# First merge's products, the gates and the head splits moved into the planned part of a hybrid RWKV-7 and GDN layer

## The chip, the cores and the metric

The kernel runs on one core of one Trainium2 chip. The metric is the device time of one execution in microseconds. Engines are named PE (TensorE), DVE (VectorE), ACT (ScalarE), POOL (GpSimd) and SP (SyncE, which here only issues DMAs).

## The reference

One layer over 256 latent tokens x and 256 context tokens ctx, of width 2048, in fp32. Both are normed and modulated by rows of an adaLN product (c with a 2048 x 12288 matrix), go through one input projection, and then through two token mixers: RWKV-7 (16 heads of 64, in both directions) and a gated DeltaNet (GDN; 8 heads of 128, chunks of 64, in both directions). Context only gives the scans their first state. Then the merge, the projection and the FFN:

```python
h = modulate(rmsnorm(x, norm1_w), sh1, sc1); hc = modulate(rmsnorm(ctx, norm1_w), csh1, csc1)
o_a = rwkv_readout(scans over h @ w_in, started from those over hc @ w_in)
o_b = gdn_readout(scans over h @ w_in, started from those over hc @ w_in)
g_a, g_b = split(h @ w_in[gate columns])
m = sigmoid(g_a) * (o_a @ p_a) + sigmoid(g_b) * (o_b @ p_b)
x = x + gt1 * (m @ w_out)
x = x + gt2 * swiglu(modulate(rmsnorm(x, norm2_w), sh2, sc2), w_gate_up, w_down)
return rmsnorm(x, final_norm_w)
```

## The kernel before

**Products.** Each big fp32 product is three in fp32r: the weights are loaded (`wraw`), ACT casts them to `whi`, DVE subtracts to get `wlo`, and PE multiplies whi with the high and the low part of the activations and wlo with the high part. A block of weights is 128 columns by 2048 rows, in four quarters of 256 KB (128 partitions x 512). Of such blocks there are 24 for the RWKV pairs (k, r, v for each of 8 pairs of heads), 24 for the GDN heads (K, V, Q), and 40 gates "g" (8 for the GDN readout, 32 for the merge).

**Stages.** (1) Norms, adaLN's first blocks and modulation write h: `H2` (line 441), two tiles (high, low) that hold latent and context tokens side by side, so that a product over both has 512 columns (k, v, K, V) and one over the latents 256 (r, Q, g). (2) A part whose order is planned: RWKV pairs (grams, inverse, values, scan), then GDN heads (features, tokens, decays, grams, inverse, scan), with the products as filling between. (3) First merge: p_a's 16 products (lines 1680 to 1696). (4) Second merge: p_b's 16 (lines 1705 to 1716). (5) w_out, FFN, last norm.

**What sets the order.** In (2) the class `Weave` writes the order of PE, DVE, ACT and POOL by a table of costs (`Lane.product`, line 117): pieces of work are generators with a rank, and where PE would have to wait for a chain's step the next of the products stands there. `products()` keeps the list of blocks; GATES_A and GATES_B say how many gates come free after each RWKV pair and each head. A block's weights are asked for at the start of the product before it (`weights`, `fetch`, `cast`). SP's row, all loads with few exceptions, is put in order by the scheduler; SP takes it in order, and a load waits there until its buffer is free. Inverses turn their blocks by storing to DRAM and loading again (`scr`, `tscr`; stores of LT, iv and extra).

**adaLN's rest** (`ada_rest`, `row_tile`): 80 tiles of 512 KB in two buffers `aw`, loaded by POOL's queue (`g.dma_start`), each added to `acc` by two instructions of 128x512 on DVE (150 in all, ten more on ACT); after 16 tiles a sum `ada_sum` goes through PE. The second merge begins behind these in PE's row, with some of its products ahead of the last sum.

**Merge.** Gates are written to DRAM (`gts_`, line 1143) and loaded again as one tile of 4 MB (line 1690) after the last one; ACT takes their sigmoid (line 1695) while p_a's products run, POOL multiplies the first merge's results with the first 16 (line 1712), DVE the second's with the others (line 1714).

## Time and profile before

| | us |
|---|---|
| median of 3 runs | 2246.44 |
| least and most of them | 2244.85, 2249.73 |
| profiled execution, time | 2257.04 |
| its span | 2254.4 |
| PE busy in it | 2132.3 |
| DVE busy in it | 1552.8 |
| ACT busy in it | 1120.9 |
| POOL busy in it | 102.1 |

The profile is of one execution; its span runs from the first to the last instruction, and 2.6 us lie around it. In its rows an engine's line number is the line of the kernel, but nearly all that the planner writes has line 160, where `Weave` records an operation; there a group is known by its tiles, out first ("wlo<-wraw,whi"). Busy times of matmuls overlap one another, since they are pipelined; their spacing, not their length, says what they cost. A clock of 0.98 is the share of full speed that was granted to PE.

### The profile page before, as it was taken

To read this page: it belongs to the slowest core of one execution; us is meant where nothing else is said; L and a number is where in the kernel's file an instruction comes from. 1 tells how busy PE (TensorE), PEld (TensorE's weight loads), DVE (VectorE), ACT (ScalarE), POOL (GpSimd) and SP (SyncE) were. 2 spreads that over 40 slices of the span, in tenths; PEclk is the share of its full clock that TensorE was granted. 3 is DMA by queue.
4 is the path that set the end of the run, shared out by engine and by line. 5 is a ranking of instruction groups with operands and counts; after the bars stand their busy time and mean duration, and the time that the engine had idled before them with its cause. 6 is when DMAs were issued, how large, how long until landed. Compare 5 with 4: busy or idle time off the path is not lost.

```text
span 2254.4 us, 55503 instructions
## 1 busy us (share of the span) xinstructions
PE 2132.3 (95%) x22906; PEld 1906.1 (85%) x22906; DVE 1552.8 (69%) x3245; ACT 1120.9 (50%) x2157; POOL 102.1 (5%) x167
## 2 busy tenths in 40 slices
PE   7998999899999999999999888999999999999998
PEld 4776677678888777888888887989999999999997
DVE  3457588888888668898887767665666665545554
ACT  3246554456545666565654463454444444444443
POOL 0000000000000001111110040000000000000000
PEclk9999999899999999999999898999999999999999
DMA  9966765454443425556667965663777776666665
GB/s 385 414 164 192 203 171 136 121 144 127 112 126 107 105 70 155 157 169 174 181 179 238 292 224 196 216 214 119 241 238 240 237 241 225 196 188 196 193 194 165
DMA packets 260253, 430.83 MB, mean 191 GB/s; under 512 B 117920, under 2 KB 133280, under 8 KB 255648
## 3 DMA queue, kind: packets, MB, share of 16 engines
q1 hardware_dynamic: 234656, 360.17, 51.5%
q0 software_dynamic: 11520, 41.95, 6.1%
q10 hardware_dynamic: 13824, 25.17, 3.5%
q8 instruction: 179, 2.93, 0.5%
q14 instruction: 74, 0.61, 0.1%
HBM read 401.44 MB, written 25.77 MB: 190 GB/s over the span
## 4 chain that ended last, share of the span: by engine, by line
PE 74%; DMA 10%; DVE 7%; ACT 5%; issue 3%; SPq 0%; ACTq 0%; DVEq 0%; POOL 0%; POOLq 0%
PE mm L160 22%; PE mm L433 12%; PE mm L431 12%; PE mm L432 12%; PE s L160 7%; PE pa L160 4%; PE pi L160 2%; DVE arena L160 2%; DVE wlo L160 1%; DMA wr<-wgu 1%; DMA wraw<-w 1%; PE mm L524 1%; DMA gts<-gts__1373 1%; ACT arena L160 1%; DMA aw<-ada_rest 1%
## 5 line engine op out<-in xcount | busy, mean ns | idle before, releaser
L422 DVE TENSOR_TENSOR wlo<-wraw,whi 128x1024 fp32r<-128x1024 f32 x328 | 394.3, 1203 | 319.9 <-ACT whi L421 319.2
L421 ACT CAST whi<-wraw 128x1024 fp32r<-128x1024 f32 x328 | 337.5, 1029 | 467.3 <-PE mm L432 404.9
L160 PE MATMUL mm<-hxh,wlo 128*128 128x256 f32 (+1 forms) x1376 | 462.9, 336 | 9.4 <-DVE wlo L160 9.3
L160 PE MATMUL mm<-hxh,whi 128*128 128x256 f32 (+1 forms) x1376 | 461.4, 335 | 5.9 <-ACT whi L160 5.4
L160 PE MATMUL mm<-hxl,whi 128*128 128x256 f32 (+1 forms) x1376 | 463.4, 337 | 1.2 <-issue 1.2
L433 PE MATMUL mm<-hfh,wlo 128*128 128x256 f32 x1344 | 372.1, 277 | 0.9 <-DVE wlo L422 0.8
L431 PE MATMUL mm<-hfh,whi 128*128 128x256 f32 x1344 | 371.2, 276 | 0.0
L432 PE MATMUL mm<-hfl,whi 128*128 128x256 f32 x1344 | 371.2, 276 | 0.0
L160 PEld LDWEIGHTS mm<-hxh,wlo 128*128 128x128 f32 x1376 | 263.4, 191 | 40.5 <-DVE wlo L160 14.2
L160 PEld LDWEIGHTS mm<-hxh,whi 128*128 128x128 f32 x1376 | 263.2, 191 | 29.4 <-ACT whi L160 6.1
L160 ACT CAST whi<-wraw 128x512 fp32r<-128x512 f32 x344 | 209.9, 617 | 156.8 <-PE mm L160 97.5
L160 PEld LDWEIGHTS mm<-hxl,whi 128*128 128x128 f32 x1376 | 263.1, 191 | 25.9 <-issue 5.2
L160 DVE TENSOR_TENSOR wlo<-wraw,whi 128x512 fp32r<-128x512 f32 x344 | 236.9, 691 | 68.7 <-ACT whi L160 64.4
L433 PEld LDWEIGHTS mm<-hfh,wlo 128*128 128x128 f32 x1344 | 252.4, 188 | 2.4 <-DVE wlo L422 2.2
L431 PEld LDWEIGHTS mm<-hfh,whi 128*128 128x128 f32 x1344 | 252.5, 188 | 0.0
L432 PEld LDWEIGHTS mm<-hfl,whi 128*128 128x128 f32 x1344 | 252.5, 188 | 0.0
L431 PE MATMUL mm<-za,whi 128*128 128x256 f32 x512 | 141.5, 276 | 0.0
L433 PE MATMUL mm<-za,wlo 128*128 128x256 f32 x512 | 141.3, 276 | 0.0
L432 PE MATMUL mm<-za,whi 128*128 128x256 f32 x512 | 141.3, 276 | 0.0
L160 DVE TENSOR_TENSOR arena<-arena 128x512 f32<-128x512 f32 (+17 forms) x522 | 121.7, 235 | 27.4 <-DMA arena<-scr 16.2
L160 DVE SCALAR_TENSOR_TENSOR aw<-aw,ck 128x512 f32<-128x512 f32 x150 | 110.0, 745 | 16.3 <-DMA aw<-ada_rest 9.9
L432 PEld LDWEIGHTS mm<-za,whi 128*128 128x128 f32 x512 | 96.1, 188 | 0.0
(364 smaller groups left out, 3940.4 us busy)
## 6 DMA issues: line engine op xcount, KB each, us to landing
wraw<-w SPq DMA_DIRECT2D x344, 256.0 KB, 3.2
wraw<-wgu SPq DMA_DIRECT2D x168, 512.0 KB, 4.6
aw<-ada_rest POOLq DMA_DIRECT2D x80, 512.0 KB, 4.8
aw<-ada_first SPq DMA_DIRECT2D x32, 1024.0 KB, 11.5
wraw<-wdn SPq DMA_DIRECT2D x64, 448.0 KB, 3.6
wraw<-wout SPq DMA_DIRECT2D x32, 512.0 KB, 4.4
aw<-ada_gt ACTq DMA_DIRECT2D x64, 256.0 KB, 5.2
wraw<-wdn SPq DMA_DIRECT2D x32, 512.0 KB, 3.6
```

The source lines that it names most:

```text
L160: return Op(self, cost, lambda: getattr(self.engine, name)(out, *a, **k), mode, base)
L421: S.copy(hi[:, c, :M], raw[:, c, :M])
L422: V.tensor_sub(lo[:, c, :M], raw[:, c, :M], hi[:, c, :M].bitcast(F32))
L431: E.matmul(ps, hi, Xh[:, k, :n], start=first and i == 0, stop=False)
L432: E.matmul(ps, hi, Xl[:, k, :n], start=False, stop=False)
L433: E.matmul(ps, lo, Xh[:, k, :n], start=False, stop=last and i == len(wt) - 1)
L524: E.matmul(ps[32 * g:32 * g + 32, 0:P], ckr[:, k].rearrange("p a b -> p (a b)"), aws[e, c][:, i, g], start=k == 0, stop=k == KT - 1)
```

## The change

h is kept in four tiles (latent and context, high and low: tags xh, xl, ch, cl) instead of two. A product over both kinds of tokens is now two of 256 columns with the same weights. The four tiles' memory is used again one by one: when the last K and V are done, the context's two become the first merge's inputs and results (`merge_in`: `oa` and `PA`); when the last gate is done, the latents' two become the gates (`merge_gates`: two loads of 2 MB); after p_a's last product the input becomes the GDN heads' output (`merge_heads`, head by head).

In the planned part now stand: p_a's 16 products as kind "p" (two quarters of 128x512 each, where it was 128x1024), their copies from PSUM, the gates' sigmoid, and POOL's products with them in eight pieces of 128x512. Weights are asked for at each quarter, when fewer than four quarters are ahead, instead of only at a block's start; at the last quarter of a product the next block is taken even if its turn has not come ("sure"), and then waited for. 33 of the gates may be taken from the start, three after the grams of head 6, four after those of head 7. After the last RWKV grams every third cast to wlo goes to POOL (52 of 128x512 in all). adaLN's tiles are loaded by SP's queue. x's load of 2 MB (`x1`) and the second merge's code stay where they were.

The core of the diff (the modulation's writes to the new tiles, left out, only follow their names):

```diff
@@ -25,7 +25,7 @@
-GATES_A, GATES_B = ((8, 2, 0, 2, 5, 3, 3, 0), (5, 0, 0, 0, 0, 2, 6, 4))
+GATES_A, GATES_B = ((33,0,0,0,0,0,0,0),(0,0,0,0,0,0,3,4))
@@ -116,6 +116,8 @@
+        if a[0].dtype == F32R and n == T:
+            return 0.1145, "full"
         if a[0].dtype == F32R:
             return 0.0065 + 0.000443 * n, "full"
@@ -439,9 +441,9 @@
-    hx = hx_ctx.enter_context(tc.tile_pool(name="hx", bufs=1, side="right"))
-    H2 = (hx.tile([P, KT, 2, T], F32R, name="hxh"), hx.tile([P, KT, 2, T], F32R, name="hxl"))
-    HX = tuple(t.rearrange("p k a t -> p k (a t)") for t in H2)
+    hx = hx_ctx.enter_context(tc.tile_pool(name="hx", bufs=1, side="right", reuse_waits="tile"))
+    HX, HC = (tuple(hx.tile([P, KT, T], F32R, tag=a + b, name="h" + a + b) for b in "hl") for a in "xc")
+    H2 = tuple(zip(HX, HC))
...
@@ -568,8 +570,11 @@
-                    gemm(ps[:m, :n], [(2 * e + k, w[k][0][:, o:o + m], w[k][1][:, o:o + m])], HX, n,
-                         e == 0 and k == 0, e == NE - 1 and k == 1)
+                    hi, lo = (t[:, o:o + m] for t in w[k])
+                    todo = [(a, w_, X) for w_, part in ((hi, 0), (hi, 1), (lo, 0)) for a, X in enumerate(H2[part][:n // T])]
+                    for i, (a, w_, X) in enumerate(todo):
+                        E.matmul(ps[:m, T * a:T * a + T], w_, X[:, 2 * e + k, :], start=e == k == i == 0,
+                                 stop=e == NE - 1 and k == 1 and i == len(todo) - 1)
@@ -1141,34 +1146,91 @@
         yield s.copy(g, ps[:, :T])
         weave.release(mmb)
         Q.dma_start(gts_[j], g)
+        if j == 39:
+            weave.ready("gates")
     def fetch(src, i):
-        for q in range(NQ):
+        for q in range(src.shape[1] // CG):
             raw = yield raws
             landed[i, q] = raw, weave.now + dq(raw, src[:, CG * q:CG * q + CG, :])
             weave.ready("asked", i, q)
             yield 0.0
-    def cast(i):
-        for q in range(NQ):
+    def cast(i, nq):
+        for q in range(nq):
             yield "asked", i, q
             raw, at = landed.pop((i, q))
             yield max(0.0, at - weave.now)
             hi = yield his
             yield s.copy(hi, raw)
             lo = yield los
-            yield v.tensor_sub(lo, raw, hi.bitcast(F32))
+            late.append(0)
+            yield (g if ("grams", NPAIR - 1, 1) in weave.done and (len(late) % 3 == 0) else v).tensor_sub(lo, raw, hi.bitcast(F32))
             raws.put(raw)
             casts[i, q] = hi, lo
             weave.ready("cast", i, q)
     def weights(src, i):
         weave.add(LAT['crank'], fetch(src, i))
-        weave.add(LAT['crank'], cast(i))
-    casts = {}
+        weave.add(LAT['crank'], cast(i, src.shape[1] // CG))
+    casts, late = {}, []
+    OA, OB, PA, gts = [], [], [], []
+    def both(dst, src, i, n):
+        yield s.copy(dst[0][:, i:i + n], src)
+        yield v.tensor_sub(dst[1][:, i:i + n], src, dst[0][:, i:i + n].bitcast(F32))
+    def merge_in():
+        yield "out", NPAIR - 1
+        for what in "KV":
+            yield what + "gemm", NGH - 1
+        oa = hx.tile([P, 2, 8, T], F32R, tag="ch", name="oa")
+        OA.extend((oa[:, 0], oa[:, 1]))
+        PA.append(hx.tile([P, KT, T], F32, tag="cl", name="PA"))
+        yield dq(PA[0][:, 0:8], oad.rearrange("k p t -> p k t"))
+        for i in range(0, 8, 2):
+            yield from both(OA, PA[0][:, i:i + 2], i, 2)
+        weave.ready("merge")
+    def first_merge(j, ps, last):
+        yield s.copy(PA[0][:, j], ps[:, :T])
+        weave.release(mmb)
+        weave.ready("evicted", j)
+        if last:
+            weave.ready("merged")
+    def merge_gates():
+        yield ("sides",)
+        yield ("gates",)
+        for i, tag in enumerate(("xh", "xl")):
+            gts.append(hx.tile([P, KT, T], F32, tag=tag, name="gts"))
+            w = dq(gts[i], gts_[8 + KT * i:24 + KT * i].rearrange("j p t -> p j t"))
+        yield w
+        yield "gram", NGH - 1
+        for t in gts:
+            for j in range(0, KT, 2):
+                yield s.activation(t[:, j:j + 2], t[:, j:j + 2], AF.Sigmoid)
+        yield s.preload_act_table_set(LNEXP)
+        for j in range(0, KT, 2):
+            for i in (j, j + 1):
+                yield "evicted", i
+            yield g.tensor_mul(PA[0][:, j:j + 2], PA[0][:, j:j + 2], gts[0][:, j:j + 2])
+    def merge_heads():
+        yield ("merged",)
+        t = hx.tile([P, 2, 8, T], F32R, tag="ch", name="ob2")
+        OB.extend((t[:, 0], t[:, 1]))
+        for h in range(NGH):
+            yield "gout", h
+            yield from both(OB, ob[:, h:h + 1], h, 1)
     def products():
@@ -1186,44 +1248,66 @@
         todo += [("g", p, ("prepared", p - 1, 0) if p else None) for p in range(NPAIR) for _ in range(GATES_A[p])]
         todo += [("g", h, ("gram", h)) for h in range(NGH) for _ in range(GATES_B[h])]
+        todo += [("p", j, ("merge",)) for j in range(KT)]
         def choose():
             for i, (what, p, need) in enumerate(todo):
                 if need is None or weave.done.get(need, 1e9) <= weave.now:
-                    return todo.pop(i)[:2]
+                    return todo.pop(i)
         def source(what, p):
+            if what == "p":
+                return A["pa"][p]
             return A["w128"][48 + p if what == "g" else 3 * p + "kvr".index(what) if what in "kvr" else 24 + 3 * p + "KVQ".index(what)]
-        i, nxt = 0, None
-        while todo or nxt:
-            if nxt is None:
+        i, asked, ahead = 0, 0, []
+        def ask(more, sure=False):
+            nonlocal asked
+            while todo and sum(2 if x[0] == "p" else NQ for x in ahead) < more:
                 nxt = choose()
+                if nxt is None and sure and not ahead:
+                    nxt = todo.pop(0)
                 if nxt is None:
-                    yield 0.5
-                    continue
+                    return
                 if nxt[0] == "g":
-                    nxt = "g", next(gate_next)
-                weights(source(*nxt), i)
-            what, p = nxt
-            nxt = choose()
-            if nxt is not None:
-                if nxt[0] == "g":
-                    nxt = "g", next(gate_next)
-                weights(source(*nxt), i + 1)
+                    nxt = "g", next(gate_next), None
+                weights(source(*nxt[:2]), asked)
+                ahead.append(nxt)
+                asked += 1
+        while todo or ahead:
+            ask(1)
+            if not ahead:
+                yield 0.5
+                continue
+            what, p, need = ahead.pop(0)
+            ask(NQ)
+            if need is not None:
+                yield need
             ps = yield mmb
-            n = 512 if what in "kvKV" else T
-            for k in range(KT):
+            sides = ((0, OA),) if what == "p" else ((0, HX), (1, HC))[:1 + (what in "kvKV")]
+            nk = OA[0].shape[1] if what == "p" else KT
+            for k in range(nk):
                 if k % CG == 0:
+                    ask(NQ, k == nk - CG)
                     yield "cast", i, k // CG
                     hi, lo = casts.pop((i, k // CG))
-                for j, (w, x) in enumerate(((hi, HX[0]), (hi, HX[1]), (lo, HX[0]))):
-                    yield e.matmul(ps[:, :n], w[:, k % CG], x[:, k, :n], start=k + j == 0, stop=k == KT - 1 and j == 2)
+                for j, (w, part) in enumerate(((hi, 0), (hi, 1), (lo, 0))):
+                    for a, X in sides:
+                        yield e.matmul(ps[:, T * a:T * a + T], w[:, k % CG], X[part][:, k, :], start=k + j + a == 0,
+                                       stop=k == nk - 1 and j == 2 and a == len(sides) - 1)
                 if k % CG == CG - 1:
                     his.put(hi)
                     los.put(lo)
             i += 1
+            if what != "p" and not any(x[0] != "p" for x in todo + ahead):
+                weave.ready("sides")
             if what == "g":
                 weave.add(150, gate_out(rs, p, ps))
+            elif what == "p":
+                weave.add(150, first_merge(p, ps, not todo and not ahead))
             else:
                 (hd if what in "KVQ" else pr)[p][what + "ps"] = ps
                 weave.ready(what + "gemm", p)
@@ -1632,8 +1716,7 @@
-            yield g.dma_start(w, A["ada_rest"][b, :, k, :])
-            yield 5.2
+            yield dq(w, A["ada_rest"][b, :, k, :])
@@ -1669,53 +1752,37 @@
         for h in range(NGH):
             for i, piece in enumerate((head_scan, head_inverse, head_grams, decays, tokens, features)):
                 weave.add(100 + 10 * h + i, piece(h))
+        weave.add(140, merge_in())
+        weave.add(300, merge_gates())
+        weave.add(99, merge_heads())
         weave.add(500, ada_early())
         weave.add(500, ada_rest())
         weave.tensor = e
         weave.free[e] = FIRST
         weave.run()
     rk_ctx.close()
-    hx_ctx.close()
     wstep[0] = 8
-    gates_ctx = ExitStack()
-    gp = gates_ctx.enter_context(tc.tile_pool(name="gp", bufs=1, reuse_waits="tile", side="right"))
-    PA = gp.tile([P, KT, T], F32, name="PA")
-    Q.dma_start(PA[:, 0:8], oad.rearrange("k p t -> p k t"))
-    Oa = (gp.tile([P, 8, T], F32R, name="oah"), gp.tile([P, 8, T], F32R, name="oal"))
-    for i in range(8):
-        split(Oa[0][:, i, :], Oa[1][:, i, :], PA[:, i, :])
-    gts = gp.tile([P, 32, T], F32, name="gts")
-    Q.dma_start(gts, gts_[8:40].rearrange("j p t -> p j t"))
-    for j in range(KT):
-        ps = pst(pmm, "mm")
-        gemm(ps[:, 0:T], load_w(A["pa"][j], P, 8), Oa, T)
-        S.copy(PA[:, j], ps[:, 0:T])
-        tc.keep_in_program_order(S.activation(gts[:, 2 * j:2 * j + 2, :], gts[:, 2 * j:2 * j + 2, :], AF.Sigmoid))
-    tc.keep_in_program_order(S.preload_act_table_set(LNEXP))
+    PA = PA[0]
     x1p = Places(None, arena, ("x1", KT * T, 1), ("rs", T, 1), ("ssum", T, 1), ("graw", 64, 1), ("s2", 16, 1), ("pad", 176, 1),
                  ("cb", 2048, 1), ("sq", T, 3), ("m", T, 2))
     x1 = x1p.tile([P, KT, T], F32, name="x1")
     ssum = x1p.tile([P, T], F32, name="ssum")
     Q.dma_start(x1, A["xT"])
-    for i in range(8):
-        split(Oa[0][:, i, :], Oa[1][:, i, :], ob[:, i, :])
     m_ctx = ExitStack()
     mp = m_ctx.enter_context(tc.tile_pool(name="mp", bufs=1, reuse_waits="tile"))
     M = (mp.tile([P, KT, T], F32R, name="mh"), mp.tile([P, KT, T], F32R, name="ml"))
     for j in range(KT):
         ps = pst(pmm, "mm")
-        gemm(ps[:, 0:T], load_w(A["pb"][j], P, 8), Oa, T)
-        G.tensor_mul(PA[:, j], PA[:, j], gts[:, j])
+        gemm(ps[:, 0:T], load_w(A["pb"][j], P, 8), OB, T)
         m = x1p.tile([P, T], F32, tag="m", name="m")
-        V.tensor_mul(m, ps[:, 0:T], gts[:, 16 + j])
+        V.tensor_mul(m, ps[:, 0:T], gts[1][:, j])
         V.tensor_add(m, m, PA[:, j])
         split(M[0][:, j], M[1][:, j], m)
-    gates_ctx.close()
+    hx_ctx.close()
     zap = ent(tc.tile_pool(name="zap", bufs=1, reuse_waits="tile", side="right"))
     W4 = zap.tile([P, 2, 4, KT, P], F32R, tag="za", name="w4")
     w4 = []
```

What this does to the order is shown at three places. First PE near the last RWKV steps (R, VX, Pm and LAl are small tiles of the scan; mm is a block's PSUM tile; hx, hc latents and context; rows are instructions in order, "x4" four alike). Before:

```order
L160 MATMUL s<-R_10507,Tx 64x64 x4
L160 MATMUL s<-VX,C 64x128 x2
L160 MATMUL s<-LAl,VX 64x64 x4
L160 MATMUL mm<-hxh,whi 128x512
L160 MATMUL mm<-hxl,whi 128x512
L160 MATMUL mm<-hxh,wlo 128x512
```

And now, the same step:

```order
L162 MATMUL s<-R_12347,Tx 64x64 x4
L162 MATMUL s<-VX,C 64x128 x2
L162 MATMUL s<-LAl,VX 64x64 x4
L162 MATMUL mm<-hch,whi 128x256
L162 MATMUL mm<-hxl,whi 128x256
L162 MATMUL mm<-hcl,whi 128x256
L162 MATMUL mm<-hxh,wlo 128x256
L162 MATMUL mm<-hch,wlo 128x256
```

Each product of 512 columns stands as two of 256, latents then context, and a step of the scan can now stand between the two.

Second SP's row among the heads (`scr` and `tscr` are stores and loads of an inverse, `wraw` weights, `aw` adaLN's tiles). Before:

```order
L171 DMA scr_111<-LT 64x4x64 x2
L171 DMA wraw<-w 128x512
L171 DMA scr_111<-iv 64x4x64 x2
L171 DMA wraw<-w 128x512
L171 DMA arena<-scr_111 64x16x16
L171 DMA wraw<-w 128x512 x5
L1143 DMA gts__1373<-arena 128x256
L171 DMA wraw<-w 128x512 x7
L171 DMA tscr_113<-arena 64x16x16
```

And now, at the corresponding inverse:

```order
L173 DMA scr_114<-LT 64x4x64 x2
L173 DMA scr_114<-extra 64x4x64 x2
L173 DMA wraw<-w 128x512
L173 DMA arena<-scr_114 64x16x16
L173 DMA wraw<-w 128x512 x4
L173 DMA aw<-ada_rest 128x1024 x2
L173 DMA wraw<-w 128x512 x2
L173 DMA aw<-ada_rest 128x1024 x2
L173 DMA wraw<-w 128x512 x3
L173 DMA tscr_116<-arena 64x16x16
```

adaLN's tiles, which were on POOL's queue, now stand between the weights and the inverse's own transfers.

Third PE around the scan of head 7 (TF, keg and gvt are tiles of a head's scan; oah, oal, oa the first merge's input, ob the GDN heads' output). Before:

```order
L431 MATMUL mm<-oah,whi 128x256
L432 MATMUL mm<-oal,whi 128x256
L433 MATMUL mm<-oah,wlo 128x256
L431 MATMUL mm<-oah,whi 128x256
L160 MATMUL s<-TF_10639,keg 128x128 x8
L432 MATMUL mm<-oal,whi 128x256
```

And now:

```order
L162 MATMUL mm<-oa,whi 128x256 x2
L162 MATMUL mm<-oa,wlo 128x256
L162 MATMUL s<-TF_12476,keg 128x128 x4
L162 MATMUL s<-gvt,TF_12476 128x128 x2
L433 MATMUL mm<-ob_18198,whi 128x256 x2
L434 MATMUL mm<-ob_18198,whi 128x256
L435 MATMUL mm<-ob_18198,wlo 128x256
```

The first merge's products end within that scan, and the second merge's (on `ob`) begin in it.

4 lines of the change are left out of this document (2 added, 2 removed).

## The prediction

> **What bounds the kernel now.** I read the page first: who is busy, and what the chain that ended last is made of.
>
> ```profile
> span 2254.4 us, 55503 instructions
> PE 2132.3 (95%) x22906; PEld 1906.1 (85%) x22906; DVE 1552.8 (69%) x3245; ACT 1120.9 (50%) x2157; POOL 102.1 (5%) x167
> PEclk9999999899999999999999898999999999999999
> PE 74%; DMA 10%; DVE 7%; ACT 5%; issue 3%; SPq 0%; ACTq 0%; DVEq 0%; POOL 0%; POOLq 0%
> ```
>
> TensorE (PE) is busy for 95% of the span and holds 74% of the chain, and the change leaves the arithmetic as it is. So it can gain only where PE waits or its granted clock is low. The windows show where, and that the two go together (columns: stretch, length, busy time of PE, weight load, DVE, ACT and POOL, granted clock, DMA share, GB/s). The stretches are, in order: the RWKV pairs (three rows), the heads up to the last inverse, the last head's inverse up to its scan, that scan up to the last adaLN sum, and the second merge's rest (two rows).
>
> ```profile
> 150.00:450.00 300.00, 273.66 (x3187) 208.13 (x3187) 225.14 (x512) 157.68 (x365) 9.68 (x24) 0.94 0.58 167
> 450.00:750.00 300.00, 290.45 (x4560) 241.02 (x4556) 252.23 (x631) 167.27 (x450) 8.13 (x23) 0.98 0.45 119
> 750.00:850.00 100.00, 95.05 (x1143) 74.29 (x1142) 65.48 (x159) 61.67 (x143) 4.21 (x4) 0.99 0.32 91
> 850.00:1212.00 362.00, 354.02 (x3835) 306.28 (x3834) 320.06 (x860) 219.47 (x477) 44.57 (x65) 0.99 0.60 173
> 1212.00:1308.00 96.00, 79.16 (x871) 75.30 (x870) 64.44 (x148) 40.16 (x83) 11.43 (x20) 0.87 0.86 287
> 1308.00:1382.00 74.00, 58.56 (x448) 55.33 (x447) 51.76 (x82) 37.60 (x61) 23.56 (x25) 0.89 0.67 231
> ```
>
> From 150 to 850 PE idles 26.3 + 9.6 + 5.0 = 41 us, and the clock takes 0.06 x 300 + 0.02 x 300 + 0.01 x 100 = 25 us more: 66 us that further work could fill. From 850 to 1212 it idles 8 us in 362: dense. From 1212 to 1382 it idles 16.8 + 15.4 = 32 us, and the clock takes 0.13 x 96 + 0.11 x 74 = 21. After that it is dense to the end.
>
> Next the places of single tiles (median time of one between least and most, first and last start). Each head's inverse begins with a store of LT to `scr`; its scan begins with the products of TF and keg.
>
> ```profile
> L171 SPq DMA_DIRECT2D scr<-LT x16: 590/606/950, 839.3 to 1213.3; - x16
> L160 PE MATMUL s<-TF,keg x128: 270/275/421, 897.1 to 1310.4; 128*128 128x128 f32 x128
> L160 DVE SCALAR_TENSOR_TENSOR aw<-aw,ck x150: 696/739/1222, 879.6 to 1378.1; 128x512 f32<-128x512 f32 x150
> ```
>
> Eight heads' inverses begin between 839.3 and 1213.3, so a head takes 374 / 7 = 53 us. Head 0 goes from inverse to scan in 897.1 - 839.3 = 58 us; head 7 needs until about 1310, that is 97. The adaLN rows' last add stands at 1378.1, 68 us behind head 7's scan, and the chain of waits there names what it waits for:
>
> ```profile
> 1356.14 8.63 DMA aw<-ada_rest
> 1364.79 1.43 DVE aw L160 x2
> 1366.61 3.75 DMA aw<-ada_rest
> ...
> 1372.44 4.87 DMA aw<-ada_rest
> 1377.41 0.76 DVE aw L160
> ```
>
> The last adaLN tiles are loaded, added and summed one behind the other, and PE, which has the sum in its row ahead of the second merge's products, waits.
>
> **The change part by part**, against the profiled execution: 2257.0 us, its span and 2.6 around it, 10.6 above the median of 2246.4.
>
> *First part, RWKV.* Counted in the order, 538 products of 256 columns more stand ahead of head 0's scan than before: ten gates more (33 for 23) and what comes with their places. Their price follows from the spacing of such products where they are dense (start, duration):
>
> ```profile
> 1181.35 0.28 PE L160 MATMUL mm<-hxh,wlo 128*128 128x256 f32 x1
> ...
> 1181.69 0.28 PE L160 MATMUL mm<-hxh,wlo 128*128 128x256 f32 x1
> ```
>
> Three spacings in 0.34 us: 0.1135 each, so 61 us of work moves ahead. It fills the 66 us above as far as the fillers reach each gap; bounds are 0 and 61 us hidden. The gaps lie mostly in the first 300 us, and part is waiting of fractions of a microsecond that a filler's own weights would not always meet: I take two thirds, 40 hidden, and **+21**. DVE must cast for them:
>
> ```profile
> L160 DVE TENSOR_TENSOR wlo<-wraw,whi 128x512 fp32r<-128x512 f32 x344 | 236.9, 691 | 68.7 <-ACT whi L160 64.4
> wraw<-w SPq DMA_DIRECT2D x344, 256.0 KB, 3.2
> ```
>
> Ten gates are 40 casts of 0.691 = 28 us on DVE, which is free for 75 + 48 + 35 = 158 us in those rows: no term. Their loads come out of the same 344.
>
> *Width.* 1488 products of 512 columns in the list and 240 ahead of it become two of 256. The wide ones were spaced so:
>
> ```profile
> 279.72 0.40 PE L160 MATMUL mm<-hxh,wlo 128*128 128x512 f32 x1
> ...
> 280.42 0.40 PE L160 MATMUL mm<-hxh,wlo 128*128 128x512 f32 x1
> ```
>
> Three in 0.70 us, 0.233 each against 2 x 0.1135 = 0.227: about 5 ns saved per wide product, 1488 x 5 = 7 us at most where PE is dense, nothing where it waits: **-5**. [...]
>
> *Heads 0 to 7.* Of product work, 190 us stands between the first and the last head's gram products in the order now, 219 before: 29 us moved out, into the first part and behind. PE is dense there, so it can all come off; but DVE is 88% busy in that row, and 53 us per head could become the head's own limit. Bounds 0 and -29; I take **-24**. Of DVE's casts 52 go to POOL, 36 us freed at 0.691, which helps. The other side of that:
>
> ```profile
> 918.67 1.09 POOL L160 TENSOR_TENSOR arena<-arena,C 128x512 f32<-128x512 f32 x1 [7.67 <-ACT arena L160]
> 919.13 1.18 DVE L160 TENSOR_TENSOR wlo<-wraw,whi 128x512 fp32r<-128x512 f32 x1 [0.72 <-ACT whi L160]
> ```
>
> A POOL instruction of this size takes 1.09 us, and the DVE cast that begins within it ends 0.55 us behind it and takes 1.18 instead of 0.69: DVE stands still while POOL works. [...] Such casts can then take from DVE what they give.
>
> *Head 7 from inverse to scan.* Now 97 us against head 0's 58. What stood on it:
>
> ```profile
> 1214.55 0.56 SPq L1702 DMA_DIRECT2D arena<-xT  x1
> 1278.30 20.13 DMA gts<-gts__1373
> ```
>
> The 2 MB of x is still asked for right ahead of the inverse's loads, the gates' 4 MB become two loads of 2 MB, one of which stands in SP's row between head 7's own small loads, and seven gates, where it was twelve, are still to be written before it. Bounds: 0 if the big loads keep the queues full, -39 if head 7 becomes like head 0; a little under half, **-18**.
>
> *Head 7's scan to the last sum.* Before, 28 of the 150 adds stand behind the scan's start in DVE's row, now 25; over 68 us that is 2.44 us per add. Three fewer are -7. Each tile now goes out on SP's queue, without POOL's share:
>
> ```profile
> L152 POOL DMA_DIRECT2D aw<-ada_rest x80: 527/530/720, 871.6 to 1372.4; - x80
> aw<-ada_rest POOLq DMA_DIRECT2D x80, 512.0 KB, 4.8
> ```
>
> A tile lands 4.8 us after its issue, and its two adds are 1.5; with two buffers that allows (4.8 + 1.5) / 2 = 3.15 us a tile, 12.5 tiles = 39 us: -29. Bounds -7 and -29, of which **-16**. While PE waits, two products of the second merge stand there as fillers, as before.
>
> *Behind the last sum* five products of the second merge stand ahead of it in both orders, eleven behind; nothing there changes: 0.
>
> Sum: 21 - 5 - 24 - 18 - 16 = **-42**: 2215 for the profiled execution, 2246.4 - 42 = 2204 for the median.
>
> **The rivals.**
>
> *R1, all is hidden.* The 61 us vanish (0 for +21), and heads, head 7 and the tail reach -29, -24 and -22: with the width -80, 2166. For it: room of 66 us. Against: a planner's fillers have never met every gap in these rows. 0.08.
>
> *R2, POOL holds DVE.* [...] DVE, 88% busy among the heads, then sets their pace: the heads' -24 goes, -18 left: 2228. 0.12.
>
> *R3, no gap is filled.* The moved products simply take their 61 us, since the gaps are waits on the pairs' own steps that the next weights do not meet: +40 on the sum, -2: 2244, no change. Against: the products sit in the planner's gaps one by one, and DVE and ACT have room. 0.10.
>
> *R4, slower: the adaLN tiles in SP's row.* SP takes its queue in order. A tile's load waits there until DVE has added the one that had its buffer, and behind it stand the weights of all products and the heads' inverse loads.
>
> ```profile
> SPq L171 <- DVE wlo L160: 261.7, 145, 8.4
> POOL aw L152 <- DVE aw L160: 122.7, 22, 18.3
> ```
>
> SP already waits 1.8 us at a time (261.7 / 145), while POOL's tiles waited up to 18.3 with nobody behind them. If each of the some 62 tiles ahead of head 7's scan costs such a 1.8, that is 112 us; DVE's 42 us of idle time from 850 to 1212 and some of PE's lead take half: +55, 2259. It decides from about 42 / 62 = 0.7 us a tile. Against: in DVE's row the add that each tile waits for stands ahead of the cast that the next weights wait for, for all 80, so SP would have waited for that cast anyway. 0.16.
>
> **How the numbers follow.** The forecast has 0.54; R1 0.08, R2 0.12, R3 0.10, R4 0.16. What this measurement can tell from no change is 0.2%, 4.5 us, the spread of the three runs being 4.9. Faster: 0.54 + 0.08 + 0.12 = 0.74; same 0.10; slower 0.16. The range leaves out R4 (0.16) and takes in the rest: R1's 2166 below, R3's 2244 and the 4.9 of spread above: 2166 to 2250. The forecast's own, from its terms' bounds taken half each, is 2180 to 2225.
>
> **What would show it.** Right: PE idle from 150 to the last RWKV step falls by about 40 us while the first head's inverse begins some 20 us later; heads follow each other in about 50 us; head 7 from its LT store to its first TF products takes about 80; the last add stands about 50 behind these. Wrong: SP's waits named for `aw` of a microsecond or more with PE idle on wlo behind them (R4); DVE casts of 1.2 us beside POOL ones in number and heads still at 53 (R2); PE's idle before 850 unchanged (R3). If the wide products' halves are spaced by over 0.12 us where dense, the width term falls.

## The result and the profile after

| | before | changed |
|---|---|---|
| median of 7 runs, us | 2245.98 | 2258.28 |
| least and most | 2242.78, 2249.73 | 2255.87, 2265.57 |
| profiled execution, us | 2257.04 | 2265.57 |
| its span, us | 2254.4 | 2263.5 |
| mean granted clock of PE | 0.975 | 0.973 |

The ratio is 1.0063 with a 95% interval of 1.0046 to 1.008: the changed kernel is 0.6% slower, where 1.9% faster was forecast. Both profiles are of executions above their kernel's median, by 11.1 and 7.3 us, so differences of one or two us between them say little. The page of the changed kernel:

```profile
span 2263.5 us, 59016 instructions
PE 2138.1 (94%) x24634; PEld 2004.8 (89%) x24634; DVE 1554.7 (69%) x3205; ACT 1118.8 (49%) x2168; POOL 128.8 (6%) x131
PEclk9999999999999988999999988999999999999999
PE 72%; DVE 12%; DMA 8%; ACT 4%; issue 3%; SPq 0%; POOL 0%; ACTq 0%; DVEq 0%; POOLq 0%
```

Early in the span the low digits of the clock have moved: before, one stood at the eighth slice (394 to 451 us); now there are two at the fifteenth and sixteenth (792 to 905 us). The windows of the changed kernel, in the stretches of the prediction, show the same:

```profile
150.00:450.00 300.00, 287.95 (x3784) 248.55 (x3783) 231.73 (x522) 170.14 (x384) 7.21 (x20) 0.99 0.62 185
450.00:750.00 300.00, 292.28 (x4821) 266.01 (x4820) 248.17 (x609) 163.31 (x429) 8.91 (x24) 0.99 0.46 130
750.00:850.00 100.00, 90.87 (x1262) 83.27 (x1261) 62.02 (x147) 59.49 (x140) 12.33 (x11) 0.93 0.35 103
850.00:1212.00 362.00, 340.98 (x4178) 315.03 (x4178) 305.75 (x797) 212.00 (x468) 57.69 (x45) 0.96 0.48 146
1212.00:1308.00 96.00, 86.45 (x1004) 82.27 (x1006) 76.85 (x183) 47.85 (x106) 24.49 (x15) 0.95 0.84 272
1308.00:1382.00 74.00, 52.90 (x467) 47.08 (x459) 53.16 (x88) 28.75 (x60) 17.61 (x11) 0.77 0.68 229
```

From 150 to 450 PE idles 12 us for 26 and the clock is at 0.99 for 0.94: there the moved gates did fill, some 29 us. Behind, much of it is given back: from 750 to 850 PE now idles 9 us for 5 at a clock of 0.93 for 0.99, from 850 to 1212 21 for 8 at 0.96 for 0.99, and from 1308 to 1382 21 for 15 at 0.77 for 0.89. (The stretches stay at their times while the work in them moves: 850 now lies ahead of head 0's inverse.) The places of single tiles show when. First a row of the kernel before that was not shown yet (the RWKV pairs' last gram products, the heads' first), then the same rows and those of the prediction for the changed kernel:

```profile
L160 PE MATMUL pa<-LAl,arena x512: 269/269/472, 198.9 to 734.7; 64*64 64x128 f32 x171
L160 PE MATMUL pa<-arena x96: 270/275/377, 833.4 to 1208.6; 128*128 128x128 f32 x96
```

```profile
L162 PE MATMUL pa<-LAl,arena x512: 268/269/473, 203.1 to 766.2; 64*64 64x128 f32 x171
L162 PE MATMUL pa<-arena x96: 270/275/583, 887.3 to 1239.0; 128*128 128x128 f32 x96
L173 SPq DMA_DIRECT2D scr<-LT x16: 595/607/1224, 894.3 to 1242.1; - x16
L162 PE MATMUL s<-TF,keg x128: 270/275/323, 956.9 to 1337.3; 128*128 128x128 f32 x128
L162 DVE SCALAR_TENSOR_TENSOR aw<-aw,ck x150: 702/741/1778, 927.1 to 1382.8; 128x512 f32<-128x512 f32 x150
```

Head 0's LT store: 839.3 to 894.3, +55.0. From there to head 7's: 374.0 to 347.8, -26.2. From that to the last product of TF and keg: 97.1 to 95.2, -1.9. To the last adaLN add: 67.7 to 45.5, -22.2. To the end of the span: 876.3 to 880.7, +4.4. The sum is +9.1, the difference of the two spans.

The +55 has two parts. The last RWKV gram comes 31.5 later (766.2 for 734.7), behind 44 us more of products (counted in both traces at the dense spacings of the prediction). From it to head 0's first gram, 833.4 - 734.7 = 98.7 us became 121.1: 22 us more, of which only 8.7 are further products (60.4 us of them for 51.7). PE idles 16.6 us in that stretch, where it idled 4.4, and its clock is 0.91 for 1.00. The largest hole stands at its end: from 874.3 to 895.2 no product of a block begins. The last 27 us ahead of head 0's LT store in the kernel before, and that hole in the changed one:

```profile
812.00:839.30 27.30, 27.30 (x220) 22.25 (x216) 18.37 (x39) 13.25 (x35) 1.13 (x1) 1.00 0.24 74
```

```profile
874.30:895.20 20.90, 13.02 (x101) 8.68 (x99) 13.46 (x32) 15.35 (x31) 2.36 (x2) 0.67 0.27 84
```

PE, which before had no idle time there, now waits 7.9 of 20.9 us, and the clock granted for its small products is 0.67. A second place lies earlier. The chain of waits of the two kernels at the inverse of the last RWKV pair (pi), before and changed:

```profile
766.32 2.14 PE mm L160 x9
768.46 1.19 PE pi L160 x86
769.65 1.36 PE mm L160 x5
771.01 0.30 PE pi L160 x23
771.31 0.55 issue
771.85 1.06 PE pi L160 x75
772.91 1.59 PE mm L160 x6
```

```profile
802.38 8.34 PE mm L162 x54
810.72 1.19 PE pi L162 x86
811.90 0.66 PE pa L162 x2
812.57 0.59 PE mm L162 x5
813.16 1.09 PE pi L162 x80
814.25 1.26 issue
815.51 0.30 PE pi L162 x11
815.81 6.66 PE mm L162 x42
```

Where 9 and 6 products of 512 columns stood ahead of a step of the inverse, 54 and 42 of 256 stand now, that is 27 and 21 wide ones: PE takes its row in order, and the step waits behind them. (The last of ACT's copies of `pi` ahead of the second step ends at 818.1; the step begins at 822.4.) The products are also slow: 54 x 0.1135 = 6.1 us took 8.34. The windows there show the clock (columns as above):

```profile
795.00:800.00 5.00, 1.43 (x13) 1.38 (x13) 4.09 (x15) 0.25 (x1) 0.00 (x0) 1.00 0.68 185
800.00:804.20 4.20, 4.20 (x22) 4.20 (x21) 0.50 (x2) 0.71 (x6) 0.00 (x0) 0.50 0.34 96
```

PE worked 1.43 of the 5 us to 800, waiting for DVE, and for the 4.2 us behind them the granted clock was 0.50; the products from 802.5 to 802.9 stand 0.21 us apart. So a wait of 3.6 us was followed by 2.2 us more for the 54 products; that the one made the other is the author's estimate.

### The profile page after: what moved, and what is told of

It reads as the page before. It is cut to its first block, busy times and chain, and to the rows that moved or that the text cites. A ratio compares the mean times of both kernels' runs of the same rounds, so it can differ in the third digit from the quotient of the medians.

```text
span 2263.5 us, 59016 instructions
## 1 busy us (share of the span) xinstructions
PE 2138.1 (94%) x24634; PEld 2004.8 (89%) x24634; DVE 1554.7 (69%) x3205; ACT 1118.8 (49%) x2168; POOL 128.8 (6%) x131
## 4 chain that ended last, share of the span: by engine, by line
PE 72%; DVE 12%; DMA 8%; ACT 4%; issue 3%; SPq 0%; POOL 0%; ACTq 0%; DVEq 0%; POOLq 0%
PE mm L162 23%; PE mm L435 11%; PE mm L433 11%; PE mm L434 11%; PE s L162 6%; PE pa L162 4%; DVE arena L162 3%; DVE wlo L162 2%; PE pi L162 2%; DVE aw L162 2%; DMA wr<-wgu 1%; DMA aw<-ada_rest 1%; DMA wraw<-w 1%; PE mm L526 1%; DVE wlo L424 1%
## 5 line engine op out<-in xcount | busy, mean ns | idle before, releaser
L424 DVE TENSOR_TENSOR wlo<-wraw,whi 128x1024 fp32r<-128x1024 f32 (+1 forms) x312 | 375.9, 1205 | 308.3 <-ACT whi L423 307.3
L423 ACT CAST whi<-wraw 128x1024 fp32r<-128x1024 f32 (+1 forms) x312 | 320.7, 1028 | 441.3 <-PE mm L434 398.5
L162 PE MATMUL mm<-hxh,wlo 128*128 128x256 f32 x1376 | 402.0, 292 | 7.7 <-DVE wlo L162 5.9
L162 PE MATMUL mm<-hxh,whi 128*128 128x256 f32 x1376 | 399.4, 290 | 4.5 <-issue 1.7
L162 PE MATMUL mm<-hxl,whi 128*128 128x256 f32 x1376 | 397.7, 289 | 0.0
L162 ACT CAST whi<-wraw 128x512 fp32r<-128x512 f32 x376 | 229.1, 617 | 163.8 <-DMA wraw<-w 55.6
L162 PE MATMUL mm<-hch,wlo 128*128 128x256 f32 x496 | 144.9, 292 | 0.0
L162 PE MATMUL mm<-hch,whi 128*128 128x256 f32 x496 | 144.4, 291 | 0.0
L162 PE MATMUL mm<-hcl,whi 128*128 128x256 f32 x496 | 144.3, 291 | 0.0
L433 PE MATMUL mm<-za,whi 128*128 128x256 f32 x512 | 141.8, 277 | 0.0
```

Of the source, the lines that this page charges most:

```text
L162: return Op(self, cost, lambda: getattr(self.engine, name)(out, *a, **k), mode, base)
L423: S.copy(hi[:, c, :M], raw[:, c, :M])
L424: V.tensor_sub(lo[:, c, :M], raw[:, c, :M], hi[:, c, :M].bitcast(F32))
L433: E.matmul(ps, hi, Xh[:, k, :n], start=first and i == 0, stop=False)
```

## The experiments

Ratios are to the kernel before, timed on the same chip, with 95% intervals; the changed kernel stands at 1.0063 (1.0046 to 1.008). 0.1% is 2.25 us. The first eight runs take single parts back or do them alone. In their expectations theory G is that the 33 gates are spent early and then lack as fillers, S that adaLN's tiles in SP's row stall the weights, P that POOL's casts hold DVE; K0, Q1 and K2 are the blocks K of head 0, Q of head 1 and K of head 2.

**adaLN's tiles back on POOL's queue (rival R4).**

```diff
-            yield dq(w, A["ada_rest"][b, :, k, :])
+            yield g.dma_start(w, A["ada_rest"][b, :, k, :])
+            yield 5.2
```

> The changed kernel with adaLN's tiles asked for by POOL's queue again, all else as changed. Theory S: 15 to 55 us faster than the changed kernel, with SP's waits for aw gone and PE's idle between 900 and 1240 down. Theory G: within 5 us, the first LT store still at about 890. Theory P: within 5 us, or slower, as POOL's casts and its DMA issues then share one row.

Measured 1.0098 (1.008 to 1.0116), 2274.23 us: not faster than the changed kernel, which theory S and R4 need it to be. By the ratios the move to SP's queue is worth some 0.35%, though the two intervals touch. SP does wait for `aw` now (36.5 us in 23 waits from 850 to 1250, for 11.4 in 6 before), but these waits do not set the time: R4's mechanism is wrong, though its 2259 is what the changed kernel takes.

**All casts on DVE (rival R2).**

```diff
-            yield (g if ("grams", NPAIR - 1, 1) in weave.done and (len(late) % 3 == 0) else v).tensor_sub(lo, raw, hi.bitcast(F32))
+            yield v.tensor_sub(lo, raw, hi.bitcast(F32))
```

> The changed kernel with all casts to wlo on DVE, none on POOL. Theory P: 10 to 25 us faster, heads under 48 us each, DVE's mean cast back from 710 to 691 ns. Theory G: within 5 us, the first LT store unchanged, heads 50 to 53 us. Theory S: within 5 us.

Measured 1.0036 (1.002 to 1.0052); the interval touches the changed kernel's, and theory P's 10 to 25 us do not come, though DVE's mean cast falls from 710 to 688 ns. What theory P rests on is seen in the changed kernel's trace, at a DVE instruction that begins within a cast of POOL's:

```profile
793.51 1.29 POOL L162 TENSOR_TENSOR wlo<-wraw,whi 128x512 fp32r<-128x512 f32 x1 [4.71 <-ACT whi L162]
793.59 1.35 DVE L162 SCALAR_TENSOR_TENSOR arena<-arena 128x128 f32<-128x128 f32 x1
795.47 0.28 DVE L162 SCALAR_TENSOR_TENSOR arena<-arena 128x128 f32<-128x128 f32 x1
```

The same shape takes 0.28 two instructions on: 1.07 us are lost to one cast, more than the 0.69 that a cast costs DVE. Not every instruction of DVE's is stretched so: one of 128x508 that reads `mm`, begun at 1192.56 within the cast from 1192.51 to 1193.80, took 0.74, for 0.73 beside none at 822.73. And the 52 casts on POOL do not decide the time, as the cross tests below show.

**The old lists of gates in the changed kernel, and the new lists alone in the kernel before.**

```diff
-GATES_A, GATES_B = ((33,0,0,0,0,0,0,0),(0,0,0,0,0,0,3,4))
+GATES_A, GATES_B = ((8, 2, 0, 2, 5, 3, 3, 0), (5, 0, 0, 0, 0, 2, 6, 4))
```

> The changed kernel with the old two lists of gates (23 ahead of K0, then 5, 2, 6 and 4 after the grams of heads 0, 5, 6 and 7), all else as changed. Theory G (the 33 gates that may be taken from the start are spent in gaps of the RWKV pairs, and then lack between Q1 and head 0's grams, where PE stood 21 us without a product, so the 61 us moved ahead are not hidden): head 0's first LT store comes back from 894 to about 840, heads take 53 us each again, and the whole is 10 to 25 us faster than the changed kernel. Theory S (adaLN's tiles in SP's row stall the weights): the same time within 4 us, heads and first part trade. Theory P (POOL's casts hold DVE): the same within 4 us.

Measured 0.9969 (0.9954 to 0.9985), 2242.64 us: some 0.9% under the changed kernel, as theory G had it. Head 0's LT store is at 838.9 again.

> The kernel before with only the new two lists of gates. Theory G: the first LT store moves from 839 to about 885, the heads gain some 25 us over the seven steps, and the whole is 10 to 25 us slower than before. Theories S and P: within 5 us of before, since neither adaLN's tiles nor casts are moved.

Measured 0.9986 (0.9973 to 0.9999): not slower. The new lists alone move head 0's LT store by 22 us, to 861.4, for 37 us more product work ahead of the last RWKV gram, which itself comes 17.9 later. So gates there can be hidden by about half, and G is not true of gates in general.

**Four of the 33 gates held back until the last RWKV grams.**

```diff
-GATES_A, GATES_B = ((33,0,0,0,0,0,0,0),(0,0,0,0,0,0,3,4))
+GATES_A, GATES_B = ((29,0,0,0,0,0,0,0),(0,0,0,0,0,0,3,4))
...
+        todo += [("g", 0, ("grams", NPAIR - 1, 1)) for _ in range(4)]
         todo += [("p", j, ("merge",)) for j in range(KT)]
```

> The changed kernel, but four of the 33 gates may be taken only after the last RWKV grams, at the list's end, so that they can stand between Q1 and K2; 29 from the start. Theory G: the hole of 21 us between Q1 and K2 is filled, head 0's first LT store comes at about 872 instead of 894, and the whole is 12 to 20 us faster than the changed kernel. Rival A (the stretch from the last RWKV gram to head 0's gram, 121 us for 99 before, is longer because ACT's chain is: ten table loads for six): the stretch stays at 120 or more, the four gates fill it, K0 starts 20 us earlier, and the gain is the same 15 to 20 us, but the loads stay at ten; if both the loads fall and the stretch falls, A has part of it.

Measured 0.9942 (0.9922 to 0.9961), 2238.94 us: 1.2% under the changed kernel, more than G's 12 to 20 us. The hole between Q1 and K2 is gone: from the last RWKV gram to head 0's scan the longest time without a product is 5.4 us, where it was 21.3. But the held gates did not fill it, they came one by one among heads 0 to 4; and the stretch from the last RWKV gram to head 0's fell from 121 to 97.7 us with six table loads for ten, which was rival A's sign of having part of it. G has the place and not the way.

**Weights asked for as before.**

```diff
-            ask(NQ)
+            ask(1)
...
-                    ask(NQ, k == nk - CG)
```

> The changed kernel with weights asked for one block ahead at a block's start, as before, not at each quarter; all else as changed. Theory G: within 6 us of the changed kernel, the hole between Q1 and K2 still there. Rival Q (asking at each quarter commits the next block too early, so that gates are taken where a k, r or v would soon be free): 8 to 20 us faster, with fewer than 27 gates begun when the last RWKV inverse starts.

Measured 1.0043 (1.0028 to 1.0059): no difference that counts, so rival Q falls. The hole without a product is still there, 17.8 us long.

**The halves alone, in the kernel before.**

```diff
+        if a[0].dtype == F32R and n == T:
+            return 0.1145, "full"
...
-                    yield e.matmul(ps[:, :n], w[:, k % CG], x[:, k, :n], start=k + j == 0, stop=k == KT - 1 and j == 2)
+                    for a in range(0, n, T):
+                        yield e.matmul(ps[:, a:a + T], w[:, k % CG], x[:, k, a:a + T], start=k + j + a == 0,
+                                       stop=k == KT - 1 and j == 2 and a + T == n)
```

> The kernel before with each listed product of 512 columns split into two of 256 columns, the planner's cost of such a half at 0.1145, nothing else changed. Theory G (gates spent early): within 5 us of before. Rival W (the halves cost: more weight loads between the pairs' small products, PE's share of weight loading up from 85% to 89% in the changed kernel): 8 to 20 us slower than before, and PE's span from 450 to 700 holds less work.

Measured 1.0132 (1.0109 to 1.0155), 2281.06 us. The longest wait of PE in it is for the last adaLN sum. The first line is the same wait in the kernel before, the second this one:

```profile
PE pa L160 <- DVE aw L160: 3.7, 1, 3.7
PE pa L162 <- DVE aw L162: 21.3, 1, 21.3
```

That is 17.6 of the 24.2 us between the two spans; but head 0's LT store too comes 23 us later (862.6), and heads and head 7 gain again, so it is not the whole account.

**Both together: the old gates and all casts on DVE** (the two edits above).

> The changed kernel with the old lists of gates and all casts on DVE. Theory G: as with the old gates alone, 0.3% under before, within 4 us. Theory P (POOL's casts hold DVE): another 6 us or more off, about 0.6% under before. If the casts on POOL help where DVE is busiest, 4 to 8 us slower than with the old gates alone.

Measured 0.9944 (0.9926 to 0.9963): as theory P had it, 0.25% off once more.

The next four ask whether it is the parts at all, or the order that the planner makes of them.

**The same halves in the unchanged order.** The planner counts a wide product as one, and it is emitted as two halves at its place.

```diff
...
+                    if n > T:
+                        op.call = lambda ps=ps, w=w, x=x, k=k, j=j: [
+                            E.matmul(ps[:, a:a + T], w[:, k % CG], x[:, k, a:a + T], start=k + j + a == 0,
+                                     stop=k == KT - 1 and j == 2 and a == T) for a in (0, T)][-1]
...
```

> The kernel before with its own order on every engine kept, in which each listed product of 512 columns is emitted as two halves of 256 at its place and the planner still counts it as one. Rival W (the narrow products cost by themselves): 20 to 35 us slower than before, as with the halves alone. Theory O (not the width but the order that the planner makes with halves and their cost made the 30 us): within 5 us of before, mean granted clock at 0.974 to 0.978 and not at 0.965.

Measured 1.0002 (0.9982 to 1.0023). The width costs nothing that can be measured over 1488 more products; the 1.3% of the halves alone came from the order.

**The planner's old cost in the changed kernel.** Everything of the change stays, but this:

```diff
-        if a[0].dtype == F32R and n == T:
-            return 0.1145, "full"
```

> The changed kernel with the planner's old cost of a product of 256 columns, 0.1199 for 0.1145; gates, widths, casts and queues as changed. Theory O (a good part of the time is what order the planner happens to make): 8 us or more away from the changed kernel, to either side, with another number of table loads than ten between the last RWKV gram and head 0's. Theory G alone: within 5 us of it, the long stretch and the ten loads as in the changed kernel.

Measured 0.9904 (0.987 to 0.9939), 2230.74 us: 1.6% under the changed kernel by these ratios, from two lines that execute nothing on the chip. The stretch from the last RWKV gram to head 0's takes 107.7 us with six table loads, as theory O had it.

**Gates held and casts on DVE together; eight held, casts on DVE too.** The edits above, and for eight:

```diff
-GATES_A, GATES_B = ((33,0,0,0,0,0,0,0),(0,0,0,0,0,0,3,4))
+GATES_A, GATES_B = ((25,0,0,0,0,0,0,0),(0,0,0,0,0,0,3,4))
...
+        todo += [("g", 0, ("grams", NPAIR - 1, 1)) for _ in range(8)]
```

> The changed kernel with four gates held back until the last RWKV grams and all casts on DVE. If what POOL's casts cost (about 0.25% with either list of gates so far) and what the spent gates cost are separate: 0.75 to 0.85% under before, about 2232 us. If the casts matter only by the order that comes of them: within 4 us of holding four alone, to either side.

> As with four gates held back and casts on DVE, but with eight held back and 25 from the start. Theory G (work put ahead of head 0's scan is hardly hidden there, and PE lacks fillers among the heads): the last RWKV gram some 15 us earlier again, and 2 to 10 us faster than with four held. If the first part hides what stands there as forecast: no faster, and PE's idle and low clock come back between 250 and 450.

Measured 0.9995 (0.9973 to 1.0018) and 0.9998 (0.9978 to 1.0019). The two gains do not add: with four gates held, taking the casts off POOL loses 0.5%. Holding eight is no better than holding four there; the last RWKV gram comes only 8 us earlier, but PE's idle time does not come back either (194 us busy of the 200 from 250 to 450, 195 with four), so neither theory has it whole.

The last six ask by what the cost acts.

**Costs of 0.117 and 0.1255.**

```diff
-            return 0.1145, "full"
+            return 0.117, "full"
```

> The changed kernel with the planner's cost of a 256-column product at 0.117, half of the way back to the old 0.1199. Theory N (the cost acts through one count: how many gates the plan spends ahead of K0; 33 in this order, 33 in the changed kernel, 29 with the old cost): within 6 us of the changed kernel, head 0's scan at 945 or later. Theory D (it acts through adaLN's tiles: 78 of 80 are added when head 7's scan begins in this order, 74 in the changed kernel, 80 with the old cost): 10 to 20 us faster than the changed kernel, most of it behind head 7's scan. Theory L (slack in the plan, growing with the cost): half of the 28 us of the old cost, 12 to 16 us faster.

> The changed kernel with that cost at 0.1255, as far above the old one as the change put it below. 26 gates stand ahead of K0 and all 80 tiles are added when head 7's scan begins. Theories N and D: within 6 us of the kernel with the old cost, 0.7 to 1.2% under before. Theory L: faster again by 10 us or more. If neither, and the old cost was a lucky order: 10 us or more slower than the old cost.

Measured 0.9895 (0.9875 to 0.9915), 2228.13 us, and 0.9951 (0.9933 to 0.9969), 2240.79 us. At 0.117 all 33 gates stand ahead of K0 as in the changed kernel, and it is 1.7% faster: N falls. It gains more than half of what the old cost gains, and a still higher cost loses again: L falls. At 0.1255, 10.6 us of the old cost's gain are gone, where N and D had at most 6: of what was expected, a lucky order at the old cost is what is left. D had 10 to 20 us, most of it behind head 7's scan, and gets 37 in the profile, of which 28 stand at head 0's LT store already. The rows of the kernel at 0.117:

```profile
L162 PE MATMUL pa<-LAl,arena x512: 268/270/473, 203.0 to 761.7; 64*64 64x128 f32 x171
L162 PE MATMUL pa<-arena x96: 270/275/377, 860.6 to 1226.8; 128*128 128x128 f32 x96
L173 SPq DMA_DIRECT2D scr<-LT x16: 575/608/814, 866.2 to 1233.7; - x16
L162 PE MATMUL s<-TF,keg x128: 270/275/581, 922.1 to 1308.6; 128*128 128x128 f32 x128
L162 DVE SCALAR_TENSOR_TENSOR aw<-aw,ck x150: 617/742/1780, 907.8 to 1344.6; 128x512 f32<-128x512 f32 x150
```

Up to the last RWKV gram it is like the changed kernel (761.7 for 766.2). Then the stretch to head 0's gram takes 98.9 us for 121.1, as before the change, and there is no hole: the longest time without a product is 4.4 us. (At the inverse of the last RWKV pair 36 products stand ahead of one step here too, so the piles alone do not make the 22 us.) Head 7 takes 1308.6 - 1233.7 = 75 us from its LT store for 95, and the adds end 36 behind that for 45.5. The windows of head 7 and of the tail show PE at work:

```profile
1212.00:1308.00 96.00, 88.84 (x1152) 83.57 (x1151) 77.04 (x187) 47.78 (x107) 17.88 (x13) 0.96 0.88 288
1308.00:1382.00 74.00, 65.48 (x502) 62.09 (x502) 62.48 (x103) 37.14 (x67) 18.10 (x11) 0.91 0.63 199
```

**Old cost with old gates; old cost with casts on DVE** (the edits above, two by two).

> The changed kernel with the old cost and the old lists of gates: 23 gates ahead of K0, 79 of 80 tiles added when head 7's scan begins. Theory N: as fast as with the old cost alone or faster, within 8 us below it. Theory D: within 6 us of it. If the gates as fillers are worth having when the cost leaves some of them for the heads: 5 to 12 us slower than with the old cost alone, 0.4 to 0.7% under before.

> The changed kernel with the old cost and all casts on DVE. 29 gates stand ahead of K0 and 80 tiles are added when head 7's scan begins, both as with the old cost alone, but fewer at each head before. Theory P (POOL's casts cost some 0.25%): 4 to 8 us faster than with the old cost alone. If the casts on POOL are worth something where DVE is the busy one: 4 to 15 us slower than it, heads 2 us longer each.

Measured 0.9985 (0.997 to 0.9999) and 1.0 (0.9982 to 1.0019). Under the old cost the new gates gain 0.8% where under the new cost they lose 0.9%, and the casts on POOL gain 1.0% where they lost 0.25%. So neither the gates nor the casts have one price; they have another in each order. The other parts were tried in one order only.

**Silu and table load as one step** (and the same for `ob`).

```diff
-        yield s.activation(kvq, kvq, AF.Silu)
-        yield s.preload_act_table_set(LNEXP)
+        yield [s.activation(kvq, kvq, AF.Silu), s.preload_act_table_set(LNEXP)]
...
```

> The changed kernel in which the planner sets each Silu of the GDN part and the table load behind it as one step on ACT, so that no other piece's Ln or Exp stands between them and asks for a load of its own: 34 loads in all for 36. Theory T (the stretch from the last RWKV gram to head 0's gram is long because ACT's table loads stand among the copies that the last RWKV scan waits for): ten loads there become eight or fewer, the stretch falls from 121 to 105 to 115, and the whole is 5 to 15 us faster than the changed kernel. Theory O (that stretch, and head 7's, are long by the order as a whole, the loads being a part of 3 us): the stretch within 4 us of 121 or moved by the new order either way, and no relation to the two loads.

Measured 1.0079 (1.006 to 1.0098): not faster. The loads in the stretch fell from ten to eight and it takes 120.1 us (770.2 to 890.3). T falls: two of the four loads more are gone and the stretch is 1 us shorter. The loads are a sign of the order: there are eight to ten of them in the four kernels whose stretch takes 119 to 121 us, and six in all others.

**The halves in the kernel before, at the old cost** (the halves alone without their first two added lines).

> The kernel before with its products in halves as in the run of the halves alone, but with the planner's old cost (0.1199 each, 0.2398 for a pair where it counted 0.233). In its order 66 of 80 adaLN tiles are added when head 7's scan begins, as with the halves alone; 70 before. Theory D (the tiles left decide the kernel before): slow as the halves alone, 15 to 30 us over before, with one long wait of PE for the last tiles. Theory C (the low cost itself makes a bad plan): within 6 us of before. Theory O (each order is a draw of its own, of some 10 us to either side): anywhere from 15 under to 30 over.

Measured 1.0021 (1.0009 to 1.0032). In the trace 36 of DVE's 150 adds come behind head 7's scan, much as with the halves alone (38; 30 before), but PE waits 0.3 us for the last ones and not 21.3: the count does not decide it, D falls. C's 6 us fit it, and so does O, which allowed nearly everything; but the same low cost with other gates or casts in the changed kernel gives 0.994, so the low number is bad only in some orders.

## Why the prediction was wrong

By its steps, in the order of its sum:

- **First part, RWKV: forecast +21, measured +55 at head 0's LT store.** This is the step that failed. It took two thirds of the 61 us moved ahead of head 0's scan as hidden, and the work behind the last RWKV gram as it was. The trace counts 540 products of 256 columns more ahead of that scan, again 61 us, and the scan begins 59.8 later (956.9 for 897.1): nothing was hidden in the end. Up to the last RWKV gram a good quarter was, 31.5 us for 44; the stretch behind it then grew by 22 us for 8.7 of products, with the hole of 21. Of the 66 us of room that the forecast counted from 150 to 850, 42 are still there (28.9 idle and 13 by the clock). The size of +21 itself is near what other orders get: with the new gates alone in the kernel before, 418 products more (47 us) make the scan 17.2 later and the LT store 22.1; at a cost of 0.117, 428 more (49 us) make them 24.9 and 26.9 later. What the forecast left out is that the planner orders everything behind anew.
- **Width: forecast -5, measured 0** in the same order (1.0002, from -4 to +5 us). The bound of 0 held.
- **Heads: forecast -24, measured -26.2.** Right: a head takes 49.7 us.
- **Head 7 from inverse to scan: forecast -18, measured -1.9.** Failed as well. PE still idles 13.8 of these 95 us, for 16.8 of 97. The chain of waits there now goes through ACT, which has the gates' sigmoids and a table load from 1303 to 1309 us, and a load of p_a's weights of 6.2 us; whether these make the difference was not tried. That it can be gained is shown by cost 0.117 (75 us for 97, -22).
- **Tail to the last sum: forecast -16, measured -22.2.** Right within its bounds, and by the pace: in the traces 28 adds stand behind head 7's scan for 30, at 1.6 us each for 2.3.
- **Behind the last sum: forecast 0, measured +4.4.** What makes these few us was not tried.

Between the forecast's -42 and the +9.1 of the profiles lie 51 us: the first part misses by 34 and head 7 by 16, the rest nearly cancels. R3's +61 came nearest for the first part, but its sign, PE's idle time before 850 unchanged, did not come: it fell from 41 to 29 us. R4 had the right number by chance: its own undoing does not make the kernel faster. What R2 rests on is seen (1.35 us on DVE for 0.28 beside a cast of POOL's) and is no reason: casts on POOL gain or lose by the order.

What was shown is that the order decides, and not the parts: the planner's cost alone, with every part kept, takes the time from 1.0063 to 0.9895, and the halves cost nothing in the old order. Where in the order it lies can be read off the traces, though only afterwards. The changed kernel and the fourteen that differ from it in one or two edits fall into two groups. Five are slower than before: the changed kernel, adaLN on POOL, casts on DVE, the old way of asking, Silu with its load. In these five, and in no other, PE has 17.8 to 28.6 us without a product between 865 and 900, ahead of head 0's scan, and head 0's LT store comes at 886.6 or later. In the other ten the longest such time from the last RWKV gram to that scan is 10.5 us, the store comes at 871.3 or earlier, and none is slower than before. PE's row of the five is the same up to the last RWKV gram and at least 14 us on, so the hole is a property of the order that the planner makes at a cost of 0.1145 with these lists, and not of one run. (The stretch to head 0's gram sorts them less well: it takes 119 to 121 us in four of the five, but 106 with the old way of asking.) That the hole makes the loss is argued from this sorting; holding four gates closed it and gained 1.2%, but moved much else too. What stays open is why the planner leaves it: neither the gates spent, nor the piles ahead of the inverse's steps, nor the table loads, nor the tiles left explain it over all runs. With 0.117 the whole change is worth 23.6 us, 1.05%, against the 42 forecast.

## What to carry to other kernels

Where a planner or a scheduler writes the order, a change of its numbers is a change of the whole order: here 2.5 ns in the cost of a product moved the time by 1.7%, more than taking back any other part of the change did. The prediction of such a change should take the new order as a draw, count in the order what stands on PE along the longest chain and where nothing does (here the hole ahead of head 0's scan), and give it a width of 1% to either side (the fifteen kernels with the change lie between 0.9895 and 1.0098); and before a part is kept or thrown out, it is timed at two or three neighbouring costs, since its sign can turn.

## What the runs showed of the hardware

- A lower clock stood behind waits of PE and can make a large part of a difference. In the changed kernel it was 0.50 for 4.2 us from 800.0, behind a wait of 3.6 us, and 0.51 from 817.0 to 820.4, where the longest wait ahead is the 1.26 us of the chain above; but behind 2.05 us of waiting up to 1388.6 it was 1.00. What in a wait decides it was not shown. An estimate of what the lower clock takes, too high where PE waits at the lower clock, is span x (1 - mean granted clock): 56 us before, 61 in the changed kernel, 80 with the halves alone (0.965), 42 at cost 0.117 (0.981) and 36 with the old cost (0.984). Of the 36 us between the changed kernel and the old cost's profile, 25 are this at most.
- In the unchanged order two fp32r products of 256 columns with the same weights cost what one of 512 does: 1.0002 (0.9982 to 1.0023) over 1488 such pairs.
- An ACT table load takes 1.28 us in these traces:

```profile
880.67 1.28 ACT L162 ACT_TABLE_LOAD   x1
```

- POOL's cast of 128x512 takes 1.49 us on the mean, and not the 1.09 of its product of the same size in the kernel before:

```profile
L162 POOL TENSOR_TENSOR wlo<-wraw,whi 128x512 fp32r<-128x512 f32 x52 | 77.5, 1491 | 372.8 <-ACT whi L162 300.4 <-PE pa L162 36.4 <-DVE arena L162 21.7
```
